# One hybrid decoder layer on one core: the written-out order of all five engines replaced by another order

## The chip, the cores and the metric

The program runs on one core of a Trainium2 chip. The metric is the device time of one execution, in microseconds (us). Three timed executions of the kernel before gave 1240.79, 1240.93 and 1236.97 us; their median is 1240.79 us.

The engines are named as the profile names them: PE multiplies matrices (PEld is its weight load), DVE is VectorE, ACT is ScalarE, POOL is GpSimd, and SP is SyncE, which issues all the DMA transfers of this kernel.

## The reference

One layer takes a prompt of 2048 positions and 8 decode sequences of 8 positions, all of width 1024:

```python
h = rmsnorm(x, norm_w)
q, k, v, qb, kb, vb, g_lr, gate_a, gate_b = split(h @ w_in)
q = rope(rmsnorm(q, q_norm_w), pos);  k = rope(rmsnorm(k, k_norm_w), pos)
o_a = attend(q, k, v)        # 8 heads x 64; branches (window, dilation) (128,1) (512,4) (2048,16),
                             # weighted by their softmax denominators
log_a = log_sigmoid(g_lr @ w_gate_up + b_gate) / 16
o_b, s_fin = gla_chunked(qb / 8, kb, vb, log_a, s0)     # 4 heads, key 64, value 128, causal
mixed = concat(o_a * silu(gate_a), rmsnorm(o_b, gla_norm_w) * silu(gate_b))
y = x + mixed @ w_out
```

The decode sequences attend over a cache of 2048 keys and values each. The outputs are `y` of both, the new keys and values, and the final states of the gated linear attention.

## The kernel before

**Projections.** The prompt is cut into 16 tiles of 128 positions. Each tile's normed input is held as two fp16 parts (`hl`, high and low), and each block of `w_in` too. One projection of a tile is 8 k-blocks times three fp16 products (high by high, high by low, low by high), so 24 matmuls of 512 columns into one accumulator `acc_...` (L1632). The blocks are v, q, k, then qkb, g, vb and gb. The output projection (`finish`, L1991) does the same into `Y`.

**The start.** `prep_first` norms the sample rows and the first four tiles: squares on ACT, a reciprocal root in small steps (`rsqrt`: Ln and Exp on ACT, the rest on DVE, L628 to L634), scaling (`x`, L1022), a cast (`early_ht`, L1023), its low part on POOL (L1024), and transposes on PE (`th`). `load_w` takes the maximum of each row block of a weight (`wm_v`, L1118), spreads it over the partitions with PE (`mx_v`), derives a scale (`ns_v`, L1146), and splits the weight into two fp16 parts (`w_v`, L1155 and L1156). One ACT instruction, written first in the program (L566), loads the function table that holds natural logarithm and exponential.

**Attention.** For each unit, PE makes scores (`s`, L902), DVE masks and takes the row minimum (L910), ACT takes the exponential (L913), PE transposes (`t`, L920), ACT, DVE and POOL split the result into two fp16 parts (`pt`), and PE multiplies with the values (`O`, L935). Keys come back from DRAM through DMA transposes (`kk`, L1344).

**Gated linear attention and sample attention.** Their matmuls are small. Some use a part of PE's columns: 64 columns (`sc_e`, `U`, the samples' second products) or 32 (`OS`, `R`, `O_s`), so that two or four of them stand on different column groups of the array. These are the column-tiled matmuls.

**What sets the order.** The program is traced once, which gives each engine a sequence of instructions numbered from 0. `ORDER` is a table with one list of those numbers for each engine. `in_order` (L546) makes each listed instruction depend on the one listed before it on its engine. So each engine runs exactly its list, in that order, and waits where an operand is not there; an instruction behind a waiting one waits too. Data dependencies come from the tiles as before, whatever the list. PE's list has 8019 numbers, DVE's 2014, ACT's 1731, POOL's 474 and SP's 1055. SP's list decides the order in which transfers are issued.

The numbers that the prediction speaks of:

- ACT 0 is the table load; 2, 3, 4 are square, Ln and Exp of the sample rows; 5, 6, 7 those of tile 0; 1 is the absolute value of `nw`; 8, 11, 14 are the squares of tiles 1, 2 and 3; 9 scales tile 0 and 10 casts it; 12 is a part of `hs`; 15 copies `hl_0`; 18 to 25 are the high parts of `w_v`.
- DVE 4 to 7 and 8 to 11 are the small steps of `rsqrt` for the sample rows and for tile 0; 12 to 19 are the eight maxima `wm_v`; 20 scales the sample rows; 21 and 22 end the maximum; 28 is `ns_v`.
- SP 3 to 6 and 8 to 11 bring the raw blocks of `w_v`; 1 brings `nw`; 7 and 12 bring tiles 0 and 1. SP 89 to 92 are the four key transposes of the first 512 positions; 86 and 110 are the transposes of `hl_7` and `hl_8`.

Of the kernel before, what the change touches and what calls it, by code (L numbers as in the profile page):

```python
# [53 lines left out]
        "6-8 0 2-3 1 10 4-5 9 11-25 74 90-91 75 92-93 76-77 94-99 78-79 100-111 80-89 112-113 26-33 42-46 "  # L54
        "34-41 47-65 116-129 140-146 66 147-160 67-68 161 114 69-71 162 72-73 163 130-131 115 132-139 "
        "164-212 214-218 213 219-281 286 282-283 287 284 288 285 289-295 310-312 296-298 313 299-304 314 "
        "305-309 315-387 390-392 397 426 398-399 427 404-405 428 406 433 409 434 410 435 411 440 416 441 "
        "417 442 418 447 421 448-449 422 454-455 423 456 461-463 468-470 475-477 484-486 491-493 500-502 "
        "509-511 516-518 525-527 532-534 539 546-548 557-559 564-566 571 540 572-573 541 582-584 587-589 "
        "592-594 601-603 610-612 615-617 622-624 629-634 639-641 658 646 659 647 660 665-667 670-671 648 "  # L60
        "672 651 675 652 676-677 653 682-684 689-691 694 706-708 711 695 712-713 696 716 699 717 700 718 "
        "701 723-725 730-732 735-737 742 754-756 761-763 743 766 744 767 749 768 750 771 751 772-773 "
        "778-780 785-787 792-794 799-801 806-808 811-813 818-820 827-829 836-838 843-845 852-854 861-863 "
        "866-868 873-875 884-886 891-893 898-900 388-389 393-396 400-401 909-911 916-918 407-408 412 402 "
        "413 419 403 420 424 414 425 415 921-923 930-931 429 932 939-941 944-945 443-446 946 436-439 430 "
        "457-458 431-432 464-465 459-460 466-467 450-453 489-490 494-495 471 953-955 962 514-515 519-520 "
        "963 482-483 487-488 507-508 512-513 472-474 478-481 496-499 503-506 521 964 967 542-545 968-969 "
        "567-570 972-973 535-538 560-563 522-524 528-531 549 974 574 979-980 984 550-555 575-581 597 556 "
        "590-591 595-596 985-986 613-614 618 991 598-600 604-607 585-586 992 608 993 609 619 998-999 620 "
        "1000 1003 635-638 1004 654-657 1005 981 621 625-626 642 627 643 628 644-645 649-650 1010-1012 "  # L70
        "661 1015-1017 662-664 680 1022 673-674 678-679 681 685-686 1023 668 692-693 669 697-698 1024 687 "
        "1027 688 1028-1029 702 1034-1036 703-705 714-715 721 719-720 709 1037 733-734 738-739 722 "
        "726-727 1038 710 1039 728 1040 729 752-753 757 740 758 774-777 1041 741 745-748 1042-1043 759 "
        "1044-1045 769 1046-1047 760 764-765 770 1048-1049 1056-1057 781 795-798 1058 816-817 788 782-784 "
        "802 789 821 790-791 1059 822 1060 809-810 1061 814-815 1062 823 1063-1067 803-805 824-826 "
        "830-833 1068-1071 841-842 846 834-835 847 869-870 848 871-872 839-840 859 849-851 855-856 860 "
        "876 857-858 864-865 887 877-883 888 894-897 901 889-890 919-920 924-925 902-908 926 912-915 "
        "927-928 937 942-943 947-948 929 933-936 965-966 970-971 938 960 949 961 950-952 975 956-958 "
        "1078-1080 1083 987-988 976-977 989-990 1084-1085 1006-1009 959 982 1086-1087 983 1088 1093-1095 "
        "1100-1101 1025-1026 1030-1031 1102 1105-1107 1124-1126 1131-1132 1112 1133 1054-1055 1113 1138 "  # L80
        "1114 1139 1119 1140 1120 1145 1121 1146-1147 1152-1154 1161-1163 1170-1172 1175-1177 1001 "
        "1182-1184 1193-1195 1200-1201 1072-1073 1202 1207-1209 1218-1219 1248-1250 1255 1220 1256 978 "
        "994 1225 995-997 1257 1226 1264 1227 1265 1230 1266 1231 1273 1232 1274 1239 1275 1240-1241 "
        "1280-1282 1285-1287 1296-1297 1310-1312 1321 1298 1322 1303 1323 1304 1328 1305 1329-1330 1002 "
        "1335-1337 1342-1344 1351 1013-1014 1018-1019 1352 1032 1353 1020 1052-1053 1358 1376-1378 "
        "1383-1385 1359 1392 1033 1050-1051 1360 1021 1393 1367 1394 1368 1399 1369 1400-1401 1089-1091 "
        "1406 1108-1110 1081 1074 1092 1111 1082 1075-1077 1407 1096-1098 1438 1408 1099 1439 1413 "
        "1103-1104 1440 1414 1449 1415 1450 1424 1122 1451 1425 1454 1426 1143-1144 1148-1149 1455 1431 "
        "1123 1129 1150 1127 1456 1432 1130 1151 1128 1115-1117 1134 1155 1118 1433 1461 1135 1157 1156 "
        "1462 1136-1137 1141-1142 1463 1466 1158-1160 1164-1167 1185 1467-1468 1477 1502-1503 1186 1504 "  # L90
        "1187 1478 1188 1509 1479 1510 1189-1190 1168 1196-1197 1191 1198 1192 1199 1169 1484 1178 1203 "
        "1173 1511 1179 1204 1174 1485 1180 1205 1181 1514 1206 1486 1515 1491 1516 1492 1523 1493 "
        "1524-1525 1532 1210 1533-1534 1539 1228 1253 1540 1221 1246-1247 1211 1251 1212-1213 1252 "
        "1214-1217 1235-1236 1222 1237-1238 1223 1242-1243 1229 1254 1224 1233 1258 1541 1564 1234 1259 "
        "1565 1548 1244 1566 1245 1549 1569 1550 1570 1557 1571 1558 1260 1580 1559 1581 1271 1261-1262 "
        "1272 1263 1267 1278 1299-1300 1306 1268-1269 1276 1279 1307 1277 1283 1301 1270 1288 1302 1582 "
        "1289-1290 1308 1291-1292 1284 1293 1309 1294 1587 1295 1588 1626 1589 1627 1594 1628 1595 1635 "
        "1596 1636 1605 1637 1606 1642 1324 1349-1350 1354-1355 1607 1313 1643 1314-1315 1325 1316 1612 "
        "1317 1326 1644 1318-1319 1327 1613 1320 1338 1651 1339-1340 1614 1341 1331 1356 1345 1652 1346 "
        "1332 1357 1347 1619 1348 1333 1361 1620 1653 1660 1621 1334 1362 1661-1662 1667 1363-1366 1668 "  # L100
        "1370-1373 1669 1388-1391 1381 1676 1374-1375 1409 1395 1379 1396 1382 1410 1380 1402-1403 "
        "1397-1398 1386 1411 1404-1405 1677 1387 1412 1678 1683-1685 1416 1690-1691 1417-1418 1692 "
        "1419-1420 1697-1699 1708-1709 1427-1430 1421-1423 1710 1452-1453 1434 1459-1460 1464 1457-1458 "
        "1441 1435-1437 1465 1442-1448 1715 1754-1756 1763 1487-1488 1764-1765 1770 1469-1472 1771 "
# [2301 lines left out]
```

## Time and profile before

| what | value |
|---|---|
| median of three timed executions | 1240.79 us (1236.97 to 1240.93) |
| span of the profiled execution | 1241.8 us |
| time of the profiled execution around its span | not listed apart; the median lies 1.0 us below the span |
| PE busy | 1187.4 us, 96% |
| DVE, ACT, POOL busy | 942.0, 817.9 and 544.5 us (76%, 66%, 44%) |
| mean granted PE clock | 0.998 |
| read and written in HBM | 183.02 MB and 75.24 MB |

The page has six parts: busy time by engine, the span in 40 slices, the DMA queues, the chain of work that ended last, the costliest groups of instructions with the idle time ahead of them, and the DMA issues. Beside it, views of the trace answer for one window of time: what each engine did in order, how long it was busy, and what ended each wait. In a row of such a view the bracket at the end tells how long the engine was idle before it and what released it.

### The profile page before, as it was taken

To read this page: it belongs to the slowest core of one execution; us is meant where nothing else is said; L and a number is where in the kernel's file an instruction comes from. 1 tells how busy PE (TensorE), PEld (TensorE's weight loads), DVE (VectorE), ACT (ScalarE), POOL (GpSimd) and SP (SyncE) were. 2 spreads that over 40 slices of the span, in tenths; PEclk is the share of its full clock that TensorE was granted. 3 is DMA by queue.
4 is the path that set the end of the run, shared out by engine and by line. 5 is a ranking of instruction groups with operands and counts; after the bars stand their busy time and mean duration, and the time that the engine had idled before them with its cause. 6 is when DMAs were issued, how large, how long until landed. Compare 5 with 4: busy or idle time off the path is not lost.

```text
span 1241.8 us, 26175 instructions
## 1 busy us (share of the span) xinstructions
PE 1187.4 (96%) x8942; PEld 715.1 (58%) x8942; DVE 942.0 (76%) x2457; ACT 817.9 (66%) x2184; POOL 544.5 (44%) x478
## 2 busy tenths in 40 slices
PE   4999999999999999999999899999999999999998
PEld 2444465566666656666776575645555665555543
DVE  7987779888988957668776666688999999833562
ACT  6654698789789978968865553468879864421220
POOL 0064433565647335552444456655634444501220
PEclk9999999999999999999999999999999999999999
DMA  8668956977866798789999887865773477899971
GB/s 279 224 197 229 224 153 154 228 220 201 192 187 170 201 249 288 227 233 266 267 244 245 229 245 215 233 198 185 222 258 94 154 243 243 274 349 372 399 278 50
DMA packets 235831, 283.07 MB, mean 228 GB/s; under 512 B 116193, under 2 KB 146866, under 8 KB 232626
## 3 DMA queue, kind: packets, MB, share of 16 engines
q1 hardware_dynamic: 235698, 281.40, 76.4%
q8 instruction: 71, 1.16, 0.4%
q14 instruction: 62, 0.51, 0.1%
HBM read 183.02 MB, written 75.24 MB: 208 GB/s over the span
## 4 chain that ended last, share of the span: by engine, by line
PE 52%; DVE 15%; ACT 12%; DMA 10%; issue 5%; POOL 4%; SPq 2%; POOLq 0%; DVEq 0%; ACTq 0%
PE Y L1991 9%; PE acc_k L1632 6%; PE acc_v L1632 5%; PE acc_q L1632 5%; PE acc_gb L1632 4%; ACT p L913 3%; PE t L920 3%; PE s L902 3%; PE O L935 3%; DMA k<-in_cache_k_win 2%; DMA qb<-q_d 2%; POOL pr L1487 2%; PE acc_qkb L1632 2%; PE OS L2248 2%; DVE p L910 2%
## 5 line engine op out<-in xcount | busy, mean ns | idle before, releaser
L1487 POOL TENSOR_TENSOR pr<-k,qb 128x512 f32<-128x512 f32 x128 | 167.9, 1312 | 172.4 <-DVE sck L1488 75.6
L1632 PEld LDWEIGHTS <-hr 128*128 128x128 f16 x1824 | 172.8, 98 | 111.7 <-issue 11.8
L913 ACT ACTIVATE p<-p,o 128x256 f32<-128x256 f32 (+1 forms) x384 | 172.9, 455 | 27.6 <-DVE o L910 20.8
L1632 PEld LDWEIGHTS <-hl 128*128 128x128 f16 x1248 | 119.4, 98 | 119.6 <-issue 7.4
L1991 PE MATMUL Y<-w_o,mh 128*128 128x512 f16 x768 | 180.3, 379 | 0.1
L887 POOL TENSOR_TENSOR pt<-p,pt 128x512 f16<-128x512 f32 (+1 forms) x80 | 91.4, 1142 | 123.5 <-ACT pt L884 96.2
L935 PE MATMUL O<-v,pt 128*128 128x128 f16 x1200 | 135.8, 220 | 8.4 <-DVE pt L880 2.8
L1488 DVE TENSOR_REDUCE sck<-pr 128x8 f32<-128x512 f32 x128 | 87.0, 679 | 53.9 <-POOL pr L1487 53.8
L920 PE MATMUL t<-ident,p 128*128 128x128 f32 x600 | 121.4, 280 | 5.5 <-ACT p L913 3.7
L935 PEld LDWEIGHTS <-pt 128*128 128x128 f16 x1200 | 94.9, 99 | 40.5 <-POOL pt L887 5.4
L1991 PEld LDWEIGHTS <-mh 128*128 128x128 f16 x768 | 72.3, 98 | 78.7 <-issue 4.9
L1632 PE MATMUL acc_g<-w_g,hr 128*128 128x272 f16 (+1 forms) x768 | 109.2, 276 | 2.0 <-ACT vbs L1274 1.5
L1632 PE MATMUL acc_v<-w_v,hl 128*128 128x512 f16 x384 | 110.0, 383 | 1.1 <-DVE vp L1287 0.8
L1632 PE MATMUL acc_q<-w_q,hl 128*128 128x512 f16 x384 | 109.6, 379 | 0.8 <-DVE vp L1287 0.6
L1632 PE MATMUL acc_k<-w_k,hl 128*128 128x512 f16 x384 | 108.4, 379 | 1.6 <-DVE vp L1287 1.5
L1632 PE MATMUL acc_vb<-w_vb,hr 128*128 128x512 f16 x384 | 95.2, 379 | 1.4 <-DVE so_g L1174 1.4
L910 DVE CUSTOM_DVE_ANT_0 p<-s,m3w,scl_s 128x128 f32<-128x128 f32 (+1 forms) x256 | 87.1, 394 | 9.7 <-DMA o_d<-o 4.6
L1632 PE MATMUL acc_gb<-w_gb,hr 128*128 128x512 f16 x384 | 94.1, 380 | 0.1
L920 PEld LDWEIGHTS t<-ident,p 128*128 128x128 f32 x600 | 75.4, 141 | 28.9 <-ACT p L913 14.1
L902 PE MATMUL s<-kk,qq 128*128 128x256 f16 (+1 forms) x512 | 85.1, 264 | 5.9 <-DMA kk<-kp_d 3.1
L1632 PE MATMUL acc_qkb<-w_qkb,hr 128*128 128x512 f16 x288 | 81.5, 379 | 0.1
L2033 POOL TENSOR_TENSOR oc<-oc 128x512 f32<-128x512 f32 x32 | 40.1, 1270 | 86.0 <-DVE oc L2026 67.7
(543 smaller groups left out, 2485.4 us busy)
## 6 DMA issues: line engine op xcount, KB each, us to landing
k<-in_cache_k_win SPq DMA_DIRECT2D x104, 256.0 KB
sv_b<-in_cache_v_win SPq DMA_DIRECT2D x24, 1024.0 KB
hr<-h_d SPq DMA_DIRECT2D x44, 512.0 KB
qb<-q_d SPq DMA_DIRECT2D x64, 256.0 KB
oc<-o_d SPq DMA_DIRECT2D x48, 264.0 KB
o_d<-o SPq DMA_DIRECT2D x64, 132.0 KB
x<-in_x_prompt SPq DMA_DIRECT2D x16, 512.0 KB
h_d<-hl SPq DMA_DIRECT2D x16, 512.0 KB
```

Of the source, the lines that this page charges most:

```text
L887: POOL.tensor_tensor(l, f, h, ALU.subtract)
L902: PE.matmul(s_ps[:, i * w : (i + 1) * w], q, k, start=(n == 0), stop=(n == len(prods) - 1),)
L910: DVE.tensor_tensor_reduce(s[:, sl], s_ps[:, sl], mask, neg, BIG, ALU.add, ALU.min, nmf(i))
L913: ACT.activation(s[:, sl], s[:, sl], AF.Exp, bias=nmf(i), scale=-1.0, accum_out=denf(i))
L920: PE.transpose(p_ps[:, i * P : (i + 1) * P], t["s"][:, i * P : (i + 1) * P], ident[:])
L935: PE.matmul(o_, t["pt"][:, c, (i * nb + b) * P : (i * nb + b + 1) * P], vf(i, b), start=(n == 0), stop=(n == 2 * nb - 1),)
L1487: POOL.tensor_tensor(pr[:], kt, qt, ALU.mult)
L1488: DVE.tensor_reduce(out, pr[:].rearrange("p (u k d) -> p u k d", u=2, k=4), AX.X, ALU.add)
L1632: PE.matmul(z, a_[:, k, :], w[:, p_, k, cols], start=(k == 0 and i == 0), stop=(k == KT - 1 and i == 2),)
L1991: PE.matmul(Y[:], a_[:, k, :], w_[:, part, k, :512], start=(i == 0), stop=(i == len(prods) - 1),)
L2033: eng.tensor_tensor(o_[g], o_[g], w[:, g].unsqueeze(2).to_broadcast([P, NH, HD]), ALU.mult)
L2248: PE.matmul(OS[32 * x : 32 * x + 32, 0:256], ps(x), vs_[bb][:, 256 * u : 256 * u + 256], start=(i == 0), stop=(i == 13),)
```

## The change

`ORDER` is replaced; nothing else is. The same numbers stand in each list, so the same instructions run, with the same operands. Whole groups of column-tiled matmuls were moved together when the new order was made. 6375 of PE's 8019 numbers stand at another place than before, 1513 of DVE's 2014, 1185 of ACT's 1731, 227 of POOL's 474 and 918 of SP's 1055. On PE the median shift is 3 places and the largest is 118.

The diff is one hunk over the whole table. Here are the heads of the lists:

```diff
     "PE": (
-        "6-8 0 2-3 1 10 4-5 9 11-25 74 90-91 75 92-93 76-77 94-99 78-79 100-111 80-89 112-113 26-33 42-46 "
+        "6-8 10 0 2-3 1 4-5 9 11-16 18 17 19-25 74 90-92 75 93 76 94-99 77-79 100-101 80-81 102 "
...
     "DVE": (
-        "2-3 1 4-7 12-13 8-11 20 14-16 0 17-19 21-25 27-28 26 29 69 36 31 30 37 70-71 38 32 39 52 40 "
+        "1 4 2-3 5 8 6-7 14 20 12 9 15 13 10 19 11 16-17 0 18 21-25 27-29 36 31 37-38 41 30 40 "
...
     "Activation": (
-        "0 2-7 1 8-12 18 15 19 13 20-21 14 22-23 16 24 17 25-28 32 29-30 33-35 31 44-46 36-42 47-49 43 "
+        "2-3 5 4 6-7 9 1 10 0 8 12 18 15 19 23 20-21 24 13 22 25 11 14 16-17 26 28 27 32-33 29 "
...
     "SP": (
-        "2-3 7 4-6 8-9 12 0 10 1 11 13 15 14 16-22 37-40 57 27-32 59 33-34 41-42 23 36 186 35 24 43-46 25 "
...
-        "82 80 79 140 84 81 115 85 116 157 89 88 108 86 90 107 109 87 91 136 167 112 110 92 128 137 127 "
+        "2 7 3 5-6 8 0 4 11 9 1 10 12 14 21 15 22 41 18 16 19 13 40 17 27-28 37 20 29 31 39 186 "
...
+        "88 86 90 89 108 92 91 140 107 109-110 136 115 87 157 128 137 131 112 133 167 127 129 "
```

1079 rows, old and new, of the table ORDER are left out of this document.

## The prediction, made before the changed kernel ran

> **What bounds the kernel now.** I read the page first: its busy times, its slices, the chain that ended last, and the idle time ahead of the three kinds of attention matmul.
>
> ```profile
> span 1241.8 us, 26175 instructions
> PE 1187.4 (96%) x8942; PEld 715.1 (58%) x8942; DVE 942.0 (76%) x2457; ACT 817.9 (66%) x2184; POOL 544.5 (44%) x478
> ...
> PE 52%; DVE 15%; ACT 12%; DMA 10%; issue 5%; POOL 4%; SPq 2%; POOLq 0%; DVEq 0%; ACTq 0%
> ...
> L935 PE MATMUL O<-v,pt 128*128 128x128 f16 x1200 | 135.8, 220 | 8.4 <-DVE pt L880 2.8
> ...
> L920 PE MATMUL t<-ident,p 128*128 128x128 f32 x600 | 121.4, 280 | 5.5 <-ACT p L913 3.7
> ...
> L902 PE MATMUL s<-kk,qq 128*128 128x256 f16 (+1 forms) x512 | 85.1, 264 | 5.9 <-DMA kk<-kp_d 3.1
> ```
>
> PE is busy for 1187.4 of 1241.8 us, and the change neither adds nor removes a matmul. So a new order can win only what lies in the other 54.4 us, and what PE loses inside its busy time. Next I cut the span into stages; the columns are the window, its length, and busy time (and instructions) of PE, PEld, DVE, ACT and POOL.
>
> ```profile
> 0.00:20.00 20.00, 4.63 (x28) 3.29 (x28) 11.14 (x32) 10.22 (x19) 2.51 (x7) 1.00 0.93 316
> 45.00:165.00 120.00, 114.54 (x604) 56.41 (x605) 100.42 (x211) 75.70 (x171) 51.85 (x49) 1.00 0.78 211
> 165.00:205.00 40.00, 35.56 (x304) 23.12 (x301) 30.51 (x120) 38.21 (x134) 14.47 (x14) 1.00 0.38 118
> 205.00:395.00 190.00, 189.74 (x1380) 121.58 (x1378) 164.11 (x409) 158.45 (x447) 111.31 (x84) 1.00 0.79 202
> 395.00:460.00 65.00, 59.27 (x458) 38.44 (x457) 49.34 (x138) 54.08 (x155) 26.12 (x21) 1.00 0.86 222
> 680.00:700.00 20.00, 16.05 (x131) 10.84 (x128) 11.12 (x42) 9.61 (x35) 6.94 (x6) 1.00 0.77 215
> 835.00:965.00 130.00, 125.71 (x1061) 72.87 (x1060) 117.59 (x297) 108.55 (x259) 67.46 (x69) 1.00 0.58 186
> ```
>
> The idle time sits in places: 15.4 us at the start, then 5.5, 4.4, 5.7, 4.0 and 4.3 us in five of these windows, and 0.3 us in the 190 us from 205 on, where nothing is to be had. Between the start and the end the windows shown hold 24.1 us of idle time.
>
> **The change part by part.** It adds and removes no listed instruction. I compared the two lists by number, and take four places where the trace shows a price; for the other moves I find no net sign.
>
> *1. The start.* These are the rows of the chain from the first squares to the first projection matmul.
>
> ```profile
> 0.73 1.28 ACT L566 ACT_TABLE_LOAD   x1 [0.73 <-PEq L2389]
> 4.46 1.06 ACT L975 ACTIVATE jk_s<-x_s 64x1024 bf16<-64x1024 f32 x1 [2.45 <-DMA x_s<-in_x_sample]
> 6.74 0.67 DVE L1118 TENSOR_REDUCE wm_v<-wr_v 128x1 f32<-128x512 f32 x1
> 8.78 0.29 ACT L631 ACTIVATE rr_x<-rr_x,ln_h 128x1 f32<-128x1 f32 x1
> 9.50 0.16 DVE L634 SCALAR_TENSOR_TENSOR rs<-ra_x,rr_x 128x1 f32<-128x1 f32 x1
> 13.28 0.21 ACT L1511 ACTIVATE nwa<-nw 128x8 f32<-128x8 f32 x1 [4.20 <-DMA nw<-in_norm_w]
> 14.43 1.13 ACT L1022 ACTIVATE x<-x,rs 128x1024 f32<-128x1024 f32 x1
> 15.18 0.37 PE L1074 MATMUL mx_v<-ident,w_v 128*1 128x128 f32 x1 [2.52 <-DVE w_v L1131]
> 15.60 1.06 ACT L1023 ACTIVATE early_ht<-x 128x1024 f16<-128x1024 f32 x1
> 16.73 2.12 POOL L1024 TENSOR_TENSOR early_ht<-x,early_ht 128x1024 f16<-128x1024 f32 x1 [15.81 <-ACT early_ht L1023]
> 17.12 1.76 DVE L1146 TENSOR_SCALAR ns_v<-nw,pr_v 128x8 f32<-128x8 f32 x1
> 18.91 0.72 ACT L1155 ACTIVATE w_v<-wr_v,ns_v 128x512 f16<-128x512 f32 x1 [0.95 <-DVE ns_v L1146]
> 20.60 0.61 PE L1632 MATMUL acc_v<-w_v,hl 128*128 128x512 f16 x1 [0.23 <-ACT hl L1012]
> ```
>
> Before, ACT has tile 0's factor at 9.66 us (9.50 + 0.16) but stands still 4.20 us for `nw`, and scales the tile at 14.43. The new ACT list scales tile 0 ahead of the `nw` step and of tile 1's squares: that looks like a gain. But it also moves the table load from first to tenth place, behind two Ln and two Exp that alternate. The trace shows one load, 1.28 us, hidden ahead of the wait for the sample rows; it doesn't show what is put in when that load comes late. Bounds: nothing in ACT's way (one table put in at the front, hidden as now), up to one load ahead of each of the four, 5.1 us in a row, all on ACT's path. I take the four, since with the listed load behind them nothing else in the program gives these functions a table.
>
> Then by the rows: squares of the sample rows end at 5.6, load and Ln at 7.1, tile 0's squares at 8.35, load and Exp at 9.85, load and Ln at 11.3, load and Exp at 12.9. The new DVE list puts three maxima (0.67 each) between tile 0's three small steps (0.16 each), so the factor is there at 12.9 + 2.0 + 0.5 = 15.4. Scaling ends at 16.5, the `nw` step at 16.7, the cast at 17.8. DVE still has three maxima and a small cast, to 17.6, then two small steps, so `mx_v` starts at 17.9 (15.18 before). From there to `ns_v` it was 17.12 - 15.18 = 1.94, so 19.85. Before, `ns_v` took 1.76 us and ended with POOL's early_ht (18.85); now POOL ends at 17.8 + 2.1 = 19.9, so it is hardly held: 20.0. ACT meanwhile has the listed load (to 19.1), tile 1's squares (20.3) and a copy (20.6), then `w_v`, and `hl_0` is out at 22.2. The first `acc_v` comes at 22.3 against 20.60: **+1.7 us**. Without loads in the way the same steps give a factor at 13.4 and `acc_v` at 19.8: -0.8 us. PE has the lists' work waiting from there on, so I carry the delay to the end.
>
> *2. Key transposes on SP's queue.* Times and lengths are those of issuing; the matmul row is the wait.
>
> ```profile
> 126.53 3.95 SPq L990 DMA_TRANSPOSE hl<-ht  x1
> 130.54 1.30 SPq L1344 DMA_TRANSPOSE kk<-kp_d  x1
> ...
> 138.20 5.70 SPq L990 DMA_TRANSPOSE hl<-ht  x1
> 143.95 1.30 SPq L1344 DMA_TRANSPOSE kk<-kp_d  x1
> ```
>
> ```profile
> 142.68 2.97 PE L1632 MATMUL acc_v<-w_v,hl 128*128 128x512 f16 x13
> 148.02 0.61 PE L902 MATMUL s<-kk,qq 128*128 128x128 f16 x8 [2.37 <-DMA kk<-kp_d]
> ```
>
> The last of four transposes stands behind that of `hl_8`, which held SP 5.70 us, and the first scores wait 2.37 us for it. The new list puts all four ahead of `hl_8`. After the transpose of `hl_7` (130.5), four issues of about 1.3 and a store of 0.3 end near 136, the last landing near 139 (the scores began 148.02 - 143.95 = 4.1 after the last issue, so it lands somewhat under 4 after). The scores stand 36 places earlier, with 7.9 us less of matmuls ahead, so at 145.65 - 7.9 = 137.7, plus 1.7 from the start: 139.4. I take **-2.0 us** (bounds 0 and -2.4). `hl_8` is issued no later than before, behind the third and fourth transposes, so nothing falls due there.
>
> *3. A stretch without long matmuls.* From 188 to 200 us, 84 neighbours in PE's list are attention matmuls, with no `acc` or `Y` among them; ACT, which feeds them, is busy 38.21 of 40 us there. The new list has 44 at most. PE has 4.4 us idle in that window; I take half, **-2.2 us** (bounds 0 and -4.4). The like stretch from 396 to 415 stays (150 before, 138 after), so the 5.7 us there stay.
>
> *4. Switches of tile size.*
>
> ```profile
> 1219.71 0.39 PE L1991 MATMUL Y<-w_o,mh 128*128 128x512 f16 x1
> 1220.03 0.33 PE L1968 MATMUL mt_s<-ident,mix_s 64*128 64x64 f32 x2
> ...
> 1226.89 10.53 PE L1991 MATMUL Y<-w_o,mh 128*128 128x512 f16 x48
> ```
>
> Within the last row matmuls start every 0.216 us ((10.53 - 0.39) / 47). From `Y` to the narrower `mt_s` it is 0.32: a switch costs 0.10 us. Neighbours in PE's list with different tile sizes number 320 before and 293 after; the eight `mt_s`, spread among `Y` before, stand together. 27 x 0.10 = **-2.7 us** (0 if all stood inside waits). Moving groups of column-tiled matmuls wins no more: such neighbours formed 138 runs and now form 137.
>
> The sum: +1.7 - 2.0 - 2.2 - 2.7 = -5.2; the span becomes 1236.6. The median of the timed runs lay 1.0 us below the profiled span, so the forecast is **1235.6 us**.
>
> **The rivals.**
>
> *Dear table switches.* If each of the four also empties ACT first and so costs twice its row, 2.56 us, the start loses 1.7 + 5.1 = 6.8 us, the sum is -0.1, and the time 1240.7: no change. For it: all four lie on one path, ahead of everything. Against it: the only load shown took 1.28 us and no more, though on an idle engine. The Trainium skill, "ScalarE: Activation LUTs", says in "Table-load gate" that the compiler places a load right before a call whose set isn't active, and in "What ACT_TABLE_LOAD costs" that one takes about 1283 ns and a drain about 1380 ns more, 2.66 us together. By that rule the time would be an estimated 1241.2; the trace agrees with the first figure (1.28) and shows no drain.
>
> *No table switch at all.* One table serves both functions from the front, the start gains 0.8, the sum is -7.7, and the time 1233.1.
>
> *Alternation itself costs: slower.* PE's list has 699 stretches of matmuls other than `acc` and `Y`, and the new one 1077, as many more heads that can wait for DVE, ACT, POOL or a DMA with the ready projections held behind them. Idle time ahead of `O`, `t` and `s` is 8.4 + 5.5 + 5.9 = 19.8 us, so 28 ns for each stretch now. At that price 378 more cost 10.7 us: 1246.3. It decides from 13.8 ns each (5.2 / 378). For it: three engines feed these heads, and ACT is nearly full from 165 to 205. Against it: from 205 to 395 the lists alternate often and PE idles 0.3 us.
>
> **How the numbers follow.** Forecast 0.40, dear switches 0.20, no switch 0.12, alternation 0.28. A change of under 0.3% (3.7 us) can't be told from none here. The forecast lies 5.2 us below the median and counts as faster four times in five, 0.32, else as no change, 0.08; no switch adds 0.12 to faster. Dear switches count as no change, 0.17, else as slower, 0.03; alternation is slower. So faster 0.44, same 0.25, slower 0.31. The forecast's own range is 1230 to 1240. The low end of the whole is all four bounds together (-0.8 - 2.4 - 4.4 - 2.7 = -10.3, so 1230.5) and a quarter of the rest of the idle time shown, 17.3 us, which a better fit elsewhere could take: 1226, and I go to 1224 for windows not shown. The high end is the alternation's time and a little more: 1248.
>
> **What would show it.** In the timeline of the first 25 us: more than one table load, and the first `acc_v` near 22 us (near 20 with none, near 27 with dear ones). The scores' first wait for `kk` under 1 us. PE idle in the window around 165 to 205 near 2 us. Idle ahead of `O`, `t` and `s` near 20 us in sum, not 30. The forecast is wrong if PE's idle time outside the start is not smaller by some 4 us, or if waits appear at places that I took as neutral.

## The result and the profile after

The changed kernel takes 1231.87 us (median of 7 runs, 1229.70 to 1233.52). The kernel before takes 1238.77 us in the 7 runs made beside it (1234.71 to 1240.93). The ratio is 0.994 with a 95% interval of 0.9923 to 0.9957: faster by 7 us, or 0.6%. The prediction said 1235.6 us and faster at 0.44. One of the ten executions of experiment 7 below took 6794 us, and its ratio leaves that one out.

These are the first lines of the page of the changed kernel: span, busy times, and the three groups of attention matmuls with the idle time ahead of them. Line numbers are 129 higher than before, since the table of the order is longer.

```profile
span 1230.7 us, 26121 instructions
PE 1174.5 (95%) x8942; PEld 717.4 (58%) x8942; DVE 916.5 (74%) x2457; ACT 826.2 (67%) x2189; POOL 539.2 (44%) x478
...
L1064 PE MATMUL O<-v,pt 128*128 128x128 f16 x1200 | 172.5, 220 | 5.7 <-DVE pt L1009 1.7
...
L1049 PE MATMUL t<-ident,p 128*128 128x128 f32 x600 | 135.3, 278 | 3.4 <-ACT p L1042 3.1
...
L1031 PE MATMUL s<-kk,qq 128*128 128x256 f16 (+1 forms) x512 | 106.5, 264 | 3.9 <-DVE o L1039 2.2
```

PE's idle time did not shrink: 1230.7 - 1174.5 = 56.2 us, where it was 54.4. Its busy time shrank by 12.9 us, with the same 8942 matmuls. Idle time ahead of `O`, `t` and `s` fell from 19.8 to 13.0 us. ACT has five more instructions (2189, before 2184). DVE needs 25.5 us less for the same 2457.

Some windows of the stages, after (length, then busy time of PE, PEld, DVE, ACT and POOL; behind them PE's granted clock, the DMA share and GB/s):

```profile
0.00:20.00 20.00, 3.49 (x22) 2.77 (x23) 8.20 (x29) 14.68 (x21) 2.52 (x7) 1.00 0.93 319
20.00:45.00 25.00, 18.93 (x120) 9.24 (x118) 23.23 (x45) 16.99 (x26) 0.00 (x0) 1.00 0.61 190
45.00:165.00 120.00, 119.14 (x616) 58.49 (x615) 95.33 (x220) 76.13 (x171) 48.74 (x47) 1.00 0.78 211
165.00:205.00 40.00, 37.47 (x334) 25.34 (x332) 34.01 (x129) 39.90 (x141) 14.99 (x15) 1.00 0.47 149
...
395.00:460.00 65.00, 56.52 (x437) 36.63 (x436) 49.75 (x137) 52.06 (x147) 24.47 (x18) 1.00 0.93 227
```

And the second window of the kernel before:

```profile
20.00:45.00 25.00, 24.22 (x141) 11.55 (x140) 23.96 (x54) 15.56 (x25) 0.00 (x0) 1.00 0.71 245
```

PE's idle time from 20 to 45 us rose from 0.8 to 6.1 us. From 165 to 205 it fell from 4.4 to 2.5, and from 45 to 165 from 5.5 to 0.9. From 395 to 460 it rose from 5.7 to 8.5.

**A measure by work done.** Windows of two kernels drift apart, so I compare them where PE has done the same work. From the PE rows of all traces I take for each form of matmul its shortest usual step from start to start: the 5th percentile, and the median for column-tiled ones, the lower one where traces differ. The sum over PE's whole list is 1101 us of work. What a stage takes beyond that is lost time, whether it shows as idle or as busy. Five more kernels run below have the order of before in all but one place (late load, fourth key transpose, 165 to 205 us, tile groups, score sums); where one of them was edited in a stage, it is left out there. Their range tells how much a stage varies from one execution to the next.

```
work done (us)    before  same order    after   load in   old start kept
                           as before             front     to 62 us
time at 20         40.6   39.8 - 41.3    47.7     44.2      41.1
lost   20- 112      5.2    4.2 -  5.5     1.6      1.6       3.9
      112- 140      3.2    1.9 -  3.2     0.4      0.4       0.4
      140- 170      9.7    8.7 -  9.3     6.8      7.3       6.8
      170- 290      1.8    1.8            1.5      1.5       1.4
      290- 310      0.1    0.1            1.8      0.9       0.9
      310- 410     11.9   12.0 - 13.9    14.0     13.9      14.0
      410- 590     12.9   12.4 - 14.2    10.3     12.7       9.9
      590- 674      8.5    3.7 -  6.5     5.2      4.3       2.7
      674- 705      3.8    2.6 -  3.8    -0.5     -0.5      -0.5
      705- 780      9.9    9.7 - 10.7     6.8      6.7       6.6
      780- 815      5.6    6.0 -  6.1     8.4      8.5       4.8
      815-1082     41.3   41.4           40.6     39.2      39.5
     1082-1101      1.7    1.7            0.4      0.4       0.4
last matmul      1237.0 1231.0-1235.1  1226.0   1222.0    1213.1
```

(A stage can come out a little under zero, since column-tiled steps are taken at their median.) Two things stand out. About half of the stages repeat to some tenths of a us wherever the order is the same; the others move by 1 to 2 us. And the profiled execution of before was itself a long one: it lost 8.5 us from 590 to 674, where its order loses 3.7 to 6.5 otherwise.

**The granted clock.** The table does not separate one more thing. In most of these traces PE is granted half its clock for 3.4, 6.8 or 10.2 us at a time, and a matmul of 512 columns then starts every 0.427 us instead of 0.216. These are such windows in experiments 1, 11, 9, 3 and 4:

```profile
27.30:30.72 3.42, 3.30 (x15) 1.72 (x15) 3.42 (x6) 3.26 (x4) 0.00 (x0) 0.50 0.93 289
29.72:36.54 6.82, 6.31 (x36) 3.86 (x37) 6.82 (x11) 3.35 (x5) 0.00 (x0) 0.50 0.33 102
34.53:41.36 6.83, 6.02 (x34) 3.83 (x35) 6.83 (x11) 2.84 (x5) 0.00 (x0) 0.50 0.40 125
48.10:54.92 6.82, 5.17 (x13) 1.90 (x14) 5.78 (x17) 4.71 (x8) 0.00 (x0) 0.50 0.26 98
882.40:892.60 10.20, 10.20 (x35) 6.75 (x34) 7.21 (x21) 4.94 (x11) 4.91 (x5) 0.50 0.64 209
```

Such a window costs up to half its length, and less where PE would have waited anyway. The profiles of before and after have one each, 3.4 us near 570 us, so it does not bear on their difference. The kernel with the load in front has that one too, besides the one at its start. The kernel with the old start to 62 us has none, and its profiled execution was the fastest of its six (1219.75 us, where the median is 1225.56): its column shows that order at its best. The five windows begin within 1.2 us of the end of a wait of PE of 1.1 to 2.9 us, but other waits of that length have none behind them (2.37 and 2.59 us in the profile of before). What sets one off, and whether the order does, is not shown.

### The profile page after: what moved, and what is told of

Same layout as the page of the kernel before. It is cut to its first block, busy times and chain, and to the rows that moved or that the text cites. A ratio compares the mean times of both kernels' runs of the same rounds, so it can differ in the third digit from the quotient of the medians.

```text
span 1230.7 us, 26121 instructions
## 1 busy us (share of the span) xinstructions
PE 1174.5 (95%) x8942; PEld 717.4 (58%) x8942; DVE 916.5 (74%) x2457; ACT 826.2 (67%) x2189; POOL 539.2 (44%) x478
## 4 chain that ended last, share of the span: by engine, by line
PE 45%; DVE 8%; ACT 4%; DMA 3%; issue 2%; POOL 1%; SPq 1%; ACTq 0%; POOLq 0%; DVEq 0%
PE Y L2120 11%; PE acc_g L1761 6%; PE acc_vb L1761 5%; PE acc_qkb L1761 4%; PE acc_gb L1761 4%; PE OS L2377 2%; PE O L1064 2%; PE t L1049 2%; PE s L1031 2%; PE sc_e L875 1%; DMA o_d<-o 1%; PE tm L2085 1%; DVE kq_e L846 1%; DVE Sbd L1940 1%; ACT qbd L834 1%
## 5 line engine op out<-in xcount | busy, mean ns | idle before, releaser
L2120 PE MATMUL Y<-w_o,mh 128*128 128x512 f16 x768 | 187.7, 379 | 0.2 <-DVE xr L2127 0.2
L1064 PE MATMUL O<-v,pt 128*128 128x128 f16 x1200 | 172.5, 220 | 5.7 <-DVE pt L1009 1.7
L1049 PE MATMUL t<-ident,p 128*128 128x128 f32 x600 | 135.3, 278 | 3.4 <-ACT p L1042 3.1
L1064 PEld LDWEIGHTS <-pt 128*128 128x128 f16 x1200 | 105.7, 99 | 49.8 <-POOL pt L1016 4.6
L1761 PE MATMUL acc_g<-w_g,hr 128*128 128x272 f16 (+1 forms) x768 | 118.7, 277 | 0.9 <-DVE so_g L1303 0.6
L1031 PE MATMUL s<-kk,qq 128*128 128x256 f16 (+1 forms) x512 | 106.5, 264 | 3.9 <-DVE o L1039 2.2
L1039 DVE CUSTOM_DVE_ANT_0 p<-s,m3w,scl_s 128x128 f32<-128x128 f32 (+1 forms) x256 | 90.7, 394 | 19.9 <-PE s L1031 10.4
L1761 PE MATMUL acc_vb<-w_vb,hr 128*128 128x512 f16 x384 | 102.2, 379 | 0.0
L1761 PE MATMUL acc_qkb<-w_qkb,hr 128*128 128x512 f16 x288 | 85.1, 379 | 0.0
L2162 POOL TENSOR_TENSOR oc<-oc 128x512 f32<-128x512 f32 x32 | 36.3, 1152 | 101.7 <-DVE oc L2155 96.0
```

Source lines behind the costliest of these rows:

```text
L1031: PE.matmul(s_ps[:, i * w : (i + 1) * w], q, k, start=(n == 0), stop=(n == len(prods) - 1),)
L1039: DVE.tensor_tensor_reduce(s[:, sl], s_ps[:, sl], mask, neg, BIG, ALU.add, ALU.min, nmf(i))
L1049: PE.transpose(p_ps[:, i * P : (i + 1) * P], t["s"][:, i * P : (i + 1) * P], ident[:])
L1064: PE.matmul(o_, t["pt"][:, c, (i * nb + b) * P : (i * nb + b + 1) * P], vf(i, b), start=(n == 0), stop=(n == 2 * nb - 1),)
L1761: PE.matmul(z, a_[:, k, :], w[:, p_, k, cols], start=(k == 0 and i == 0), stop=(k == KT - 1 and i == 2),)
L2120: PE.matmul(Y[:], a_[:, k, :], w_[:, part, k, :512], start=(i == 0), stop=(i == len(prods) - 1),)
```

## The experiments

Ratios are to the kernel before, with a 95% interval.

### 1. The load back in front

```diff
 "Activation":
-    2-3 5 4 6-7 9 1 10 0 8 12 ...
+    0 2-3 5 4 6-7 9 1 10 8 12 ...
```

> The changed kernel with one edit: the table load back at the front of ACT's list (0 ahead of 2). Theory: the five loads of 1.28 us that came in with the late load are on ACT's path to tile 0's factor (four of them) and ahead of the third squares (the listed one). Without them there is one load, the factor is there near 10 us instead of 14.8, the first acc_v comes near 18 us instead of 21.35, and the time falls by 3 to 4 us against the changed kernel: about 1228, ratio to the kernel before 0.991. Rival: the late start comes from the new order of ACT's and DVE's lists itself (squares of tiles 2 and 3 behind the w_v pieces, a w_v piece behind the factor of three tiles), and the loads lay beside waits for DMA: then first acc_v moves by under 1.3 us and the time by about 1 us, to 1231.

Measured: 0.9916 (0.9895 to 0.9938), span 1226.7. This is ACT of the changed kernel:

```profile
0.73 1.28 ACT L1104 ACT_TABLE_LOAD   x1 [0.73 <-PEq L2518]
...
5.48 1.28 ACT L758 ACT_TABLE_LOAD   x1
6.78 0.20 ACT L758 ACTIVATE rr_xs<-rv_xs 64x1 f32<-64x1 f32 x1
...
8.04 1.28 ACT L760 ACT_TABLE_LOAD   x1
...
9.55 1.28 ACT L758 ACT_TABLE_LOAD   x1
...
11.07 1.28 ACT L760 ACT_TABLE_LOAD   x1
12.36 0.29 ACT L760 ACTIVATE rr_x<-rr_x,ln_h 128x1 f32<-128x1 f32 x1
14.80 1.15 ACT L1151 ACTIVATE x<-x,rs 128x1024 f32<-128x1024 f32 x1 [2.14 <-DVE rs L763]
...
17.05 1.28 ACT L695 ACT_TABLE_LOAD   x1
```

Six loads, one of them ahead of anything: five more than before, each 1.28 us, with the next instruction right behind (6.78 after 5.48 + 1.28 = 6.76). With the load in front there is one; tile 0 is scaled at 11.51 instead of 14.80 us, the first `acc_v` starts at 17.85 instead of 21.35, and at 20 us of work 3.5 of the 7.1 us are back. The theory holds. The other 3.6 us hold the new order itself and up to 1.7 us of the halved clock from 27.30 on, which the profile of the changed kernel does not have there.

### 2. The late load alone

```diff
 "Activation":
-    0 2-7 1 8-12 ...
+    2-7 1 8-9 0 10-12 ...
```

> The kernel before with one edit: the table load in tenth place of ACT's list, as in the changed kernel. Theory: six loads of 1.28 us again. Four of them fall into the 4.20 us for which ACT waits for nw there, so only the listed one, now ahead of tile 0's cast, is on the path: cast, POOL's half and hl_0 come 1.3 us later, first acc_v near 21.5 instead of 20.60, time up by about 1 us (ratio 1.001). Rival, dear loads (2.56 us each with a drain): ten more us of ACT ahead of the cast, of which some 4 hide: first acc_v near 27, time up by 6 us, ratio 1.005.

Measured: 1.0011 (0.9996 to 1.0026). ACT again has six loads; these rows show where they went:

```profile
13.76 0.21 ACT L1640 ACTIVATE nwa<-nw 128x8 f32<-128x8 f32 x1 [0.87 <-DMA nw<-in_norm_w]
...
16.07 1.28 ACT L695 ACT_TABLE_LOAD   x1
17.36 1.06 ACT L1152 ACTIVATE early_ht<-x 128x1024 f16<-128x1024 f32 x1
```

Four loads fit into the wait for `nw` (4.20 us before, 0.87 left). Only the listed one is on the path. At 20 us of work it costs 1.7 us against the profile of before, of which some 0.5 is `nw` itself, read at 13.76 instead of 13.28; on the whole time the cost can't be told from none. The price of a load depends on what ACT would have waited for anyway. Dear loads fall.

### 3 and 4. Whole stretches exchanged

For the first, all five lists begin with what the kernel before starts in its first 42 us and go on in the new order. For the second, the new order has the old one for what lies between 640 and 800 us.

> All five lists begin with what the kernel before starts in its first 42 us, in its order, and go on in the changed kernel's order. Theory: the changed order loses its time at the start only there (PE has done the first 20 us of its work at 47.7 us instead of 40.6, and 5.3 us of that are left at 80 us); with the old start this is won back: span about 1225, time about 1226, ratio 0.990, the fastest of the three. Rival: what is won later depends on the later start (work prepared in the meantime, DMAs that come in time), and the waits come back: then the time stays near 1231.

> The changed kernel with the order of the kernel before, in all five lists, for what lies between 640 and 800 us. Between these places PE of the changed kernel gains 9 to 10 us on the kernel before (from +0.1 to -9.6 at equal work done). Theory: the gain is made there by the order there, so it is lost again: time about 1240, ratio 1.001. Rival: it is made by what was prepared earlier in the changed order (earlier loads and finished operands), so that most of it stays: about 1233, ratio 0.995.

Measured: 0.9939 (0.9917 to 0.9960) and 1.0019 (1.0000 to 1.0038). The old start is level at 20 us of work (41.0), but loses 4.7 us in the next five, at the seam, where the one order passes into the other:

```profile
47.83 0.38 PE L1206 MATMUL mx_k<-mm_k,one_row 1*128 1x1 f32 x2 [2.88 <-DVE mm_k L1205]
```

DVE's new list puts a `w_q` piece ahead of that maximum, and the piece waits for ACT. Right behind this wait PE's clock is halved from 48.10 to 54.92, with 21 `acc_v` in most of it, so the seam did not make all of the loss. The theory's 0.990 is not reached, but this run says little on the start; experiment 10 goes on from it.

The exchange in the middle gives gain back: it loses 3.8 us from 674 to 705, as before, where the new order loses nothing (-0.5). From 705 to 780, with the second seam near 720, it loses 7.8 (after 6.8, before 9.9). The 12.8 us that it loses from 780 to 815 lie behind the stretch: 5.1 of them are the halved clock from 882.40 to 892.60, with PE busy all through, and the changed kernel loses 8.4 there too. So the order there makes all of the first stage's gain, and the time of this run overstates what was given back. For the second stage the run doesn't decide, since a seam lies in it.

### 5. The fourth key transpose alone

```diff
 "SP":
-    ... 91 136 167 112 110 92 128 ...
+    ... 91 92 136 167 112 110 128 ...
```

> The kernel before with one edit on SP's list: the fourth key transpose (92) moved from behind hl_8's transpose (110) to right behind the third (91). Theory (the prediction's second step): the first scores waited for it alone; their wait of 2.37 us for kk goes and nothing falls due behind, hl_8's users included: 2.4 us less where PE has done 120 us of its work, and about 0.2% on the whole time, ratio 0.998. Rival: hl_8's transpose, 1.3 us later now, is waited for by acc_v further on, or the transposes slow each other: under 0.5 us of it is left at 160 us of work, ratio 1.000.

Measured: 0.9985 (0.9968 to 1.0002). The PE rows of this kernel:

```profile
144.26 0.61 PE L1031 MATMUL s<-kk,qq 128*128 128x128 f16 x8
...
147.08 0.33 PE L1049 MATMUL t<-ident,p 128*128 128x128 f32 x1 [0.59 <-ACT p L1042]
```

The wait of 2.37 us ahead of the first scores is gone, and the first transposes now wait 0.59 us for ACT. From 112 to 140 us of work this kernel loses 1.7 us; the unedited ones lose 1.9 to 3.2. So the move alone gives between 0.2 and 1.5 us, not 2.4; theory (0.998) and rival (1.000) both lie inside the interval. In the changed kernel no wait is left there:

```profile
130.41 2.63 SPq L1473 DMA_TRANSPOSE kk<-kp_d  x2
133.72 3.46 SPq L1473 DMA_TRANSPOSE kk<-kp_d  x2
141.95 1.79 SPq L1119 DMA_TRANSPOSE hl<-ht  x1
```

```profile
141.18 0.33 PE L1031 MATMUL s<-kk,qq 128*128 128x128 f16 x3
```

Its scores come one to three at a time among projections, and 0.4 us are lost in the stage. So other moves have a share in it.

### 6. The stretch from 165 to 205 us alone

All five lists of the kernel before, with the new order for what lies between 165 and 205 us.

> The kernel before with the changed order, in all five lists, for what lies between 165 and 205 us alone. Theory (the prediction's third step): long matmuls put between the attention matmuls cover the waits there; the changed kernel gained 2.8 us between 140 and 170 us of work done, so 2 to 3 us less, ratio 0.998. Rival: the gain there came from what was done earlier in the changed order (the kernel with the late load alone also gained 1.0 there): then under 1 us, ratio 1.000.

Measured: 0.9996 (0.9977 to 1.0015). From 140 to 170 us of work it loses 6.8 us, as the changed kernel does, where the order of before loses 8.7 to 9.7 in five executions (one of them with its clock halved for 3.4 us there): 2 to 3 us gained, made by the order there. Behind its seam it loses 2.8 instead of 1.8, and the total can't be told from none.

### 7. Tile sizes and column halves alone

```diff
 "PE":
-    4384-4385 4394 4396 4386-4387 4395 4388-4391 ... 4397
+    4384-4391 4394-4397
...
     (the eight mt_s, 7931 to 7938, in two runs of four instead of six runs)
```

> The kernel before with two edits on PE's list alone: the eight O_s matmuls and behind them the four U_s (column tiles of 64, in the order left, right, left, right) put together at 770 us, where they stood as O_s, O_s, U_s left, U_s left, O_s, O_s, U_s right, O_s x4, with the last U_s 10 us later; and the eight mt_s at 1217 to 1221 put into two runs of four from six. Theory by the changed kernel's trace: two U_s of unlike column halves run beside each other, 0.43 us per matmul against 0.90, so 2 us less at 770 and not nothing, as the prediction's fourth step had it; mt_s 0.8 us less by 0.10 us per switch (eight fewer). In all 2.5 to 3, ratio 0.998. Rival: what U_s gives is taken back by the readers of U_s and O_s; and a switch has no price of its own, 0: ratio 1.000.

Measured: 0.9979 (0.9961 to 0.9998). First the kernel before, then this one:

```profile
770.59 0.62 PE L1857 MATMUL O_s<-S,qxs 128*32 128x256 f32 x4
771.15 1.93 PE L1890 MATMUL U_s<-vx,kdt_smp 64*64 64x512 f32 x4
773.00 0.63 PE L1857 MATMUL O_s<-S,qxs 128*32 128x256 f32 x4
773.56 1.07 PE L1890 MATMUL U_s<-vx,kdt_smp 64*64 64x512 f32 x2
```

```profile
768.00 1.92 PE L1986 MATMUL O_s<-S,qxs 128*32 128x256 f32 x16
769.85 3.02 PE L2019 MATMUL U_s<-vx,kdt_smp 64*64 64x512 f32 x8
```

(An f32 matmul has two records.) Two left halves in a row take 1.93 us; four in the order left, right, left, right take 3.02. From 674 to 780 us of work the kernel loses 11.7 us, the unedited ones 12.5 to 13.8. In the last stage it loses 0.7 instead of 1.7: eight switches fewer at `mt_s` are worth 1.0 us, or 0.12 each. So `mt_s` gives what the theory said, and the first edit 0.8 to 2.1 us where it said 2. The ratio stands for 2.6 us in sum, but its interval reaches from 0.2 to 4.8.

### 8. The score sums behind the copy

```diff
 "DVE":
-    ... 828 1133 1138 ...
+    ... 1133 1138 828 ...
```

> The kernel before with one edit on DVE's list: the score sums sck (828), which wait for POOL's product pr, and this for a DMA, moved behind the probabilities' copy pt_3_12_0 and the sum o3_11 (1133, 1138) that stood behind them. Theory: of the gain between 600 and 640 us of work the greater part is this: DVE stood 3.91 us for pr with the copy for the next O ready behind it, and PE 2.59 us for that copy. The wait goes whole: 2.6 us less at 640 us of work (about 1 if the DMA comes as early as in the kernel with the late load, where DVE stood 0.99 us). Rival: PE's list is the cause (in the changed kernel 11 acc_vb more stand ahead of the next O), and with PE's list as before O only waits for the next thing, ACT's half of the copy: under 0.5 us.

Measured: 1.0002 (0.9986 to 1.0018). What it was built on stood in the profile of before, DVE and PE:

```profile
690.43 0.69 DVE L1488 TENSOR_REDUCE sck<-pr 128x8 f32<-128x512 f32 x1 [3.91 <-POOL pr L1487]
```

```profile
691.77 0.62 PE L935 MATMUL O<-v,pt 128*128 128x128 f16 x8 [2.59 <-DVE pt L880]
```

Four other kernels have the same order there. In them (experiments 2, 5, 6 and 7) DVE waits 0.99, 2.37, 1.71 and 2.46 us at this place, and PE 0, 1.05, 0.40 and 1.14. First PE in experiment 7, then PE in the edited kernel:

```profile
689.85 0.62 PE L1064 MATMUL O<-v,pt 128*128 128x128 f16 x8 [1.14 <-DVE pt L1009]
```

```profile
693.24 0.28 PE L1761 MATMUL acc_g<-w_g,hr 128*128 128x272 f16 x1 [1.68 <-DVE so_g L1303]
```

So this wait, the largest single one that the profile after lacks, belongs to the order, but its size to one execution: POOL's `pr` waited for a key transfer from DRAM that came late in it. With the edit PE no longer waits ahead of `O`, but 1.68 us further on, where it waits 0.16 us or so otherwise. The edit gives nothing: 6.4 us lost from 590 to 674, the unedited kernels 3.7 to 6.5. My theory falls. The rival's size is right (under 0.5 us), but the wait that came in its place is another than it named.

### 9 to 11. Mending the start

Experiment 9 adds three mends to the load in front: the squares of tile 2 (ACT 11) right behind those of tile 1 (8), the last `w_v` piece on DVE (42) ahead of the three tiles' factor and two maxima behind it, and the old order for 296 to 306 and 776 to 815 us of work. Experiment 10 keeps the old start to 62 us, with the same two stretches. Experiment 11 has only DVE 42 moved, behind 43.

> The changed kernel with the load at the front of ACT's list, and three mends where its trace loses against the kernel before. Start: tile 2's squares right behind tile 1's on ACT; on DVE the last w_v piece ahead of the three tiles' factor, and two maxima behind it (PE stood 2.19 us for that piece, and then for the three tiles' casts). And the order of the kernel before, in all lists, from 296 to 306 and from 776 to 815 us of work done (the changed kernel loses 1.7 and 2.4 us there, at a first score ahead of its kk and at heads that wait for DVE). Theory: each loss is where its waits are, so the start gives 1.5 to 2 us more than the load alone and the two stretches 4: time 5 to 6 us under that of the kernel with the load in front, ratio 0.987. Rival: a wait mended moves to the next head (as with the fourth key transpose, where 0.75 of 1.5 us came back): about half, ratio 0.9895.

> The start of the kernel before in all lists, kept up to 62 us (38 us of work done) instead of 42, then the changed order with the same two stretches of the kernel before. Theory: the 4.7 us that the kernel with the old start lost between 20 and 25 us of work were the seam, where the changed lists put w_q pieces on DVE ahead of the maximum mm_k that PE waited 2.88 us for; with the cut behind that place they don't come, PE is level with the kernel before at 40 us of work (+0.0 to 0.5) and the time is 1.5 us under that of the kernel with the load in front by the start, 4 by the stretches: ratio 0.987. Rival: another wait of the kind comes at the new seam: 2 to 4 us more, ratio 0.990.

> The kernel with the load in front, with one edit on DVE's list: the last w_v piece (42) from behind the three tiles' factor (35) to right behind the piece before it (43). Nothing is moved on ACT this time. Theory: with the load in front 3.6 us are still lost at 20 us of work against the kernel before; 2.19 of them are PE's wait for this piece, which stood behind a factor that waits for ACT's squares of tiles 2 and 3. The wait goes, and the waits for the casts that follow (0.66 and 1.10 us) grow by some of it, since the factor comes no earlier: 1 to 2 us less at 40 us of work. Rival: all of it comes back at the casts, under 0.5 us.

Measured: 0.9919 (0.9897 to 0.9940), 0.9882 (0.9860 to 0.9904) and 0.9905 (0.9891 to 0.9920).

In experiment 9 the second stretch gave nearly what was expected of both (780 to 815: 4.8 us lost instead of 8.5); the first gave nothing (290 to 310: 0.9 us or so lost with it and without it). But the start got worse, 50.1 us at 20 us of work, of which the halved clock from 34.53 on took up to 3.4. ACT stood for tile 2's rows, with `hs` and all of `w_v` behind, and the ratio reaches neither theory nor rival:

```profile
20.21 1.06 ACT L1104 ACTIVATE jk<-x 128x1024 bf16<-128x1024 f32 x1 [5.00 <-DMA x<-in_x_prompt]
```

In experiment 11 the wait of 2.19 us for the piece is gone, and this comes in its place:

```profile
28.52 0.23 PE L1135 MATMUL th<-ident,early_ht 128*128 128x128 f16 x1 [2.41 <-ACT early_ht L1107]
```

In the kernel with only the load in front this `th` starts at 28.82 us, so 0.3 of the 2.19 us is kept, as the rival said. At 40 us of work it is 1.1 us behind that kernel, but its clock was halved for 6.8 us in this stretch and that one's for 3.4, which makes up to 1.7; so from there on the run does not decide between theory and rival. The late start of the new order isn't one wait; by these rows it is a chain through ACT (squares of tiles 2 and 3 behind the `w_v` pieces), the factor and the casts. Experiment 10 keeps the order of before in this chain, is level with before at 20 us (41.1) and 0.6 us behind it at 40. Its ratio lies between theory (0.987) and rival (0.990) and decides for neither.

### 12. Ready matmuls ahead of waiting ones

```diff
 "PE":
-    ... 2713 2703-2704 2680 2705 2681 2714 2719-2721 2706 2732-2734 ...
+    ... 2713-2714 2719-2721 2732-2734 2703-2704 2680 2705 2681 2706 ...
...
-    ... 3667 3726-3728 3668 3696 3729-3733 4333-4338 4341-4344 ...
+    ... 3667-3668 3696 4333-4338 4341-4344 3726-3733 ...
```

> The kernel with the long old start, with two edits on PE's list alone. Six O matmuls that PE waits 1.84 us for at 427 us (their probabilities come from DVE and ACT) go behind seven ready acc_qkb (0.216 us each), and eight O matmuls waited for 1.12 us at 577 us go behind ten ready acc_g (0.11 each). Theory: a wait at a head is worth what ready long matmuls can be put ahead of it, and it is the place in PE's list that makes the wait: 1.5 us less between 375 and 410 us of work and 1.1 between 522 and 590, ratio 0.986. Rival: what ACT and DVE do next waits for these O matmuls, and the waits come again at the next heads: under half of it, ratio 0.988.

Measured: 0.9852 (0.9831 to 0.9872), span 1218.3; the interval overlaps that of experiment 10. First the waits at the two places in its parent, the kernel of experiment 10:

```profile
426.79 0.45 PE L1064 MATMUL O<-v,pt 128*128 128x128 f16 x5 [1.67 <-DVE pt L1009]
439.19 0.38 PE L1761 MATMUL acc_qkb<-w_qkb,hl 128*128 128x512 f16 x1 [0.81 <-ACT zq L1381]
```

```profile
576.71 0.37 PE L1064 MATMUL O<-v,pt 128*128 128x128 f16 x3 [0.96 <-DVE o L1081]
```

And its own:

```profile
427.85 0.55 PE L1049 MATMUL t<-ident,p 128*128 128x128 f32 x3 [0.65 <-ACT p L1042]
437.81 0.38 PE L1761 MATMUL acc_qkb<-w_qkb,hl 128*128 128x512 f16 x1 [1.73 <-ACT zq L1381]
```

```profile
575.33 1.27 PE L1761 MATMUL acc_g<-w_g,hr 128*128 128x256 f16 x10 [1.45 <-DVE za L1463]
```

From 375 to 410 us of work it loses 4.5 us, as its parent does, and from 522 to 590 it loses 3.3 against 2.4. The first wait came back as 0.65 us ahead of the next `t` and 0.92 more ahead of `acc_qkb` (0.81 in the parent); the ten `acc_g` weren't ready at all, their accumulator being read by DVE. By the stages the rival holds, though the ratio lies nearer the theory's 0.986: both show no gain, and the profiled executions of the two kernels, both without a halved clock before the last matmul, have spans of 1217.8 and 1218.3 us. That its ratio is lower than that of experiment 10 is in part the clock: 0.999 in the median of its executions, 0.997 in those of its parent. By the ratios it is the fastest kernel here, about 18 us under the kernel before (experiment 10: 15) and some 11 under the changed one.

An estimate of the clock's part: with the share of the clock that was not granted taken off each execution's time, for the kernel before as well, the ratios of experiments 1, 3, 4, 9, 10, 11 and 12 become 0.989, 0.991, 0.999, 0.991, 0.988, 0.987 and 0.986, where they measured 0.9916, 0.9939, 1.0019, 0.9919, 0.9882, 0.9905 and 0.9852. It takes off too much where PE would have waited anyway.

## Why the prediction was right, and where it was not

The verdict and the sign were right, and the time is within 4 us. The sum is right in part by luck: the start cost more than forecast and two stretches lost time unforeseen, against a gain in short gaps that was not foreseen either.

The prediction's own signs came in part. There are six loads, the first `acc_v` is at 21.35, `s` does not wait for `kk`, and the window at 165 has 2.5 us of idle time. But PE's idle time outside the first 20 us, which was to fall by some 4 us, went from 39.0 to 39.7 us (behind 45 us, from 38.2 to 33.6), and waits came at places taken as neutral (290 to 310 and 780 to 815). So the picture of waits that are filled is only half of it: the gain of the whole lies inside PE's busy time.

**1, the start: right mechanism, wrong end.** The table load that comes late brings one load per alternating Ln and Exp, 1.28 us each and nothing more. Step by step the forecast ran up to 1 us late: factor 14.8 (15.4), scaling ended 15.95 (16.5), `mx_v` 17.2 (17.9), `ns_v` out 19.4 (20.0), first `acc_v` 21.35 (22.3), so +0.75 and not +1.7. With the load in front `acc_v` came at 17.85, where the prediction had 19.8, so the loads cost 3.5 us and not the 2.5 that it gave them. What failed is the sentence that PE has the lists' work waiting from there on. It doesn't:

```profile
30.92 0.41 PE L1452 MATMUL acc_v_s<-w_v,hs 128*64 128x512 f16 x2 [2.19 <-DVE w_v L1285]
...
35.76 0.51 PE L1135 MATMUL th<-ident,early_ht 128*128 128x128 f16 x6 [1.13 <-DVE early_ht L1108]
...
38.74 0.83 PE L1135 MATMUL th<-ident,early_ht 128*128 128x128 f16 x12 [1.11 <-ACT hl L1141]
```

At 20 us of work 7.1 us are lost: by experiment 1, with its halved clock, 3.5 to 5.2 by the loads and the rest by the order of ACT and DVE behind them. Up to 112 us some 3 come back, at heads (the matmul that stands next in PE's list) that now have their operands in time.

**2, the key transposes: -2.0 in size, not in cause.** The stage lost 1.9 to 3.2 us and now loses 0.4. But the move on SP's queue alone gives 0.2 to 1.5 (experiment 5). I had put the price of the wait in full, and had not asked which wait is next.

**3, the stretch at 188 to 200: right.** -2.2 forecast; experiment 6, with the order of before all around, gains 2 to 3 in this stage, and idle time in the window is 2.5 us (near 2 forecast). The like stretch at 396 stays, as said, at 12 to 14 us for 310 to 410.

**4, the switches: right, and one line wrong.** Among PE's neighbours of different tile size, 260 showed a gap of 0.03 to 0.4 us behind the first 20 us of work, 32.2 us in all; after the change 230, with 28.7. So -3.5 where I said -2.7, at 0.12 us a gap instead of 0.10. The samples' transposes show it too, first before, then after:

```profile
751.48 0.27 PE L669 MATMUL ptg_smp<-ident,zqk_smp 64*128 64x64 f32 x1
751.90 0.27 PE L669 MATMUL ptg_smp<-ident,zqk_smp 64*128 64x64 f32 x1
752.33 0.27 PE L669 MATMUL ptg_smp<-ident,zqk_smp 64*128 64x64 f32 x1
```

```profile
742.36 0.35 PE L798 MATMUL ptg_smp<-ident,zqk_smp 64*128 64x64 f32 x3
```

What failed is "moving groups of column-tiled matmuls wins no more". I had counted runs of such neighbours, 138 and 137, and not the order inside a run. `U_s` in the order left, right fell from 7.1 to 5.1 us for its eight, each taken from its start to the next matmul's.

**Not foreseen.** Between neighbours of full size, gaps of 0.03 to 0.4 us fell from 21.4 us (189 gaps) to 13.7 (124); in the five other kernels with the old order they are 21.7 to 23.0. The largest part is `t` behind `t`, 42 gaps with 4.9 us, then 14 with 1.0. Such a `t` waits for ACT's next `p`, and in the new list another matmul stands in that place. These waits are too short to show as idle time; they lie inside PE's busy time, and their 7.7 us are the largest part found of the 12.9 by which that fell. No edit isolates this gain; that alternation makes it is argued from the traces. The slower rival priced each more alternating head at 28 ns; idle time ahead of `O`, `t` and `s` fell to 13.0 us where it said 30, so it falls.

Against this stand losses: 1.7 us at 290 to 310 (the first scores of a block now ahead of their `kk`) and 2.4 or more at 780 to 815. The old order there undoes the second (experiments 9 and 10). It does not undo the first: 0.9 us are lost with it, as in the kernel with the load in front without it.

**The other rivals.** Dear loads fall by the rows of ACT: nothing lies between a load and its function. The Trainium skill, "ScalarE: Activation LUTs", says in "What ACT_TABLE_LOAD costs" that a drain of about 1380 ns goes with each load; ten such loads in two kernels (the changed one and experiment 2) show 1.28 us alone, and the measurement decides. By that rule the estimate in the prediction comes to 1241.1, not 1241.2. No switch at all falls too.

**Span and median.** I took the median 1.0 us under the span. The profiled execution was not one of the three timed ones: the timed run that goes with the new profile (1232.75) lies 2.05 us above its span. So the profile of before was of an execution of about 1244 us, long by some 5, and its spans are no measure of the gain: 11.1 us by them, 6.9 by the medians.

## What to carry to other kernels

Before pricing a wait from one profile, see how long it is in a second execution: the largest one here kept PE 2.59 us, and 0 to 1.14 us in four others. Compare the granted clock of the two executions stage by stage before a loss is put down to an order. A wait taken away is worth what the next head on that engine doesn't wait, so follow the chain one step further (the four edits of that kind, experiments 5, 8, 11 and 12, gave between nothing and 1.5 us), while a cost inside the engine, such as a switch of tile size, was won by one list alone (experiment 7). Keep an explicit table load first, and look at alternating functions whenever it moves.

## What the hardware showed that I had not expected

- A load of a function table late in ACT's list makes the program carry one load for each alternation ahead of it: six at 1.28 us (one ahead of anything, four for the two Ln and two Exp, and the listed one), although one at the front serves both functions (experiments 1 and 2).
- A switch of tile size on PE costs 0.10 us into the smaller and 0.14 out of it at `ptg_smp`, 0.12 on average. The Trainium skill, "TensorEngine Tiling (Array Packing)", says in "Key Properties" that changing the tiling mode drains the engine; the trace agrees in so far as a switch costs time, and this is the price, though it does not show the drain itself.
- The same DVE instruction can take many times as long: `ns_v` 1.76 us before, beside POOL's `early_ht`, and 0.23 after, when POOL was ending. The Trainium skill, "SBUF — State Buffer", says in "SBUF: two separate sides" that the two share a pair of ports that one of them holds for a whole instruction; the trace agrees (before, `ns_v` ends at 18.88 us and `early_ht` at 18.85). The largest part of DVE's 25.5 us less busy time looks alike (twelve `rv_qk` 15.8 us, then 7.6); that the rest is of this kind, and what PE gained by it, is not shown.
- PE was granted half its clock for 3.4 to 10.2 us at a time in 12 of the 14 executions profiled here while it had matmuls to do, and matmuls of 512 columns then started every 0.427 us instead of 0.216 (experiments 1, 3, 4, 9 and 11).
